# A hybrid mLSTM / HGRN2 decoder layer on one core: HGRN2 levels two to a step, a written order at the beginning, fewer products in the forget sums, a longer held tail

## The chip, the cores and the metric

The kernel runs on one core of a Trainium2 chip. The metric is the device time of one execution in microseconds, the median of several. The engines are named as in the profile: PE (matrix products and transposes; PEld is its weight load), DVE (vector), ACT (scalar), POOL (GpSimd) and SP, whose queue issues nearly all DMAs. Each engine takes its instructions in order.

## The reference, cut to what matters

One layer, 512 tokens, width 1024, all float32. One projection `x @ w_in` feeds two mixers; their gated sum goes through `w_out` and a layer norm, then a SwiGLU block (hidden 2816) and a second layer norm.

```python
def reference(...):
    u = x @ w_in[layer] + b_in[layer]
    (mq, mk, mv, mo, mi, mf, hq, hf, hi, hg, ga, gb) = jnp.split(u, split_points, axis=-1)
    h_a = _mlstm_chunkwise(...)        # 4 heads x 512, forget gate: running sum of log f over time
    h_b = _hgrn2_chunkwise(silu(hq), -expm1(log_f), hi, log_f)   # 8 heads x 128
    mixed = sigmoid(ga) * (h_a @ w_proj_a) + sigmoid(gb) * (h_b @ w_proj_b)
    x = _layernorm(ALPHA * x + mixed @ w_out, ln1_g, ln1_b)
    ffn = (silu(x @ w_ffn_gate) * (x @ w_ffn_up)) @ w_ffn_down
    x = _layernorm(ALPHA * x + ffn, ln2_g, ln2_b)

# HGRN2:  S_t = diag(f_t) S_{t-1} + k_t v_t^T,  k_t = 1 - f_t,  o_t = S_t^T q_t
```

## The kernel before

**Large products.** Every large product is made of three matmuls in a rounded float32 type (`mm3`: high by high, high by low, low by high), 128 x 512 each. `load_w` fetches a 512 KB piece of a weight into one of five `wraw` buffers, `split_w` makes its high part on ACT (`whi`) and its low part on DVE (`wlo`), in three buffers each. One projection (`proj_sub`) is 24 matmuls into one PSUM bank.

**Deferred work.** The rest of the computation is cut into pieces that are put between projections: `defer(n, fn)` keeps a piece back, `tick(w)` counts projections and runs what is due. The tool that builds the program then orders the instructions of each engine; `issue_after` and `keep_in_program_order` bind it.

**The beginning.** SP loads x as four row tiles `xn` with two pieces `rawv` of the value weights between them; PE transposes all four tiles (32 transposes, through PSUM tiles `px` and `s0` to `s2`), ACT and DVE split them into `xh` and `xl`, then `natural_part` makes the first values for four row tiles (96 matmuls of 264 columns).

**The mLSTM forget sums.** `gates_1` to `gates_4` run between the first projections. `gates_2` sums `lf` over time with ten float32 products of four columns (`tri` for a row tile itself, `ones` for each one before it); `gates_4` turns a running maximum (`mrow`) and makes the decay tables `dt`.

**HGRN2.** Two heads at a time (a pair, four in all), `h_units` makes f, K, Q and the output gate `og` by projections. `h_chain` then builds the scores by levels hs = 1, 2, 4, ... 256: at a level the keys of the lower half of each block of 2 hs tokens meet the queries of the upper half (`h_chunks` or the branches of `h_level`), `h_advance` multiplies the decay into half of Q and of K in place, and DVE's `copy_predicated` or ACT's copy puts the scores into `adc`, `ad`, `a1`, `a2`. The steps are due at 0 (the diagonal), 0.5, 1.25, 2, 2.75, 3.5, 4, 4.5, 5 and 5.5 ticks, the outputs (`h_out`) at 6 and 6.5. All these matmuls are float32, each two instructions in the trace: 32 x 32 or 32 x 16 in four column positions of the array for the diagonal and levels 1 to 16 (32 matmuls each), 32 x 32 in two positions for level 32 (16), 64 x 64 in one position for level 64 (8).

**The end.** `natural_pass` runs the last product for row tiles 2 and 3 over 22 weight rows k. The last three are held back (`tail=3`), so that the four PSUM banks end one after the other; `ln_stats` and `ln2_out` then do the layer norm by halves e of a row tile, one half of tile 2 on ACT and POOL.

## Time and profile before

| | us |
|---|---|
| median of 3 runs | 1318.94 (1315.4 to 1318.94) |
| the profiled execution, whole | 1315.66 |
| its span | 1313.9 |
| PE busy | 1297.1 (99%) |
| DVE busy | 709.9 (54%) |
| ACT busy | 528.5 (40%) |

The profiled execution takes 1.8 us outside the span; it is 3.3 us shorter than the median and close to the shortest run. PE's busy time counts pipelined instructions from their start to a modelled end, so a stall of a fraction of a microsecond shows in the distance from one start to the next and not as idle time. A 128 x 512 matmul starts 0.227 us after the one before it in the steady stretches.

### The profile page before, as it was taken

Reading aid. Unit: us, or ns where it says so; the run is one execution under the profiler, and the core shown is the slowest. Engines: PE = TensorE matmul, PEld = TensorE weight load, DVE = VectorE, ACT = ScalarE, POOL = GpSimd, SP = SyncE. Lnnn points to the kernel's source line nnn. Section 1 sums busy time; section 2 is a strip of 40 time slices with the busy share of each in tenths; the row PEclk is TensorE's granted clock in tenths of the full one; section 3 lists DMA queues with packets and bytes.
Section 4 is the critical chain, followed back from the end, with each engine's and each line's share of the span. In section 5 each row is a group of like instructions: output and inputs, shape, how many; then the busy total and the mean of one; then the engine's idle time right before and its main releaser. Section 6 shows DMA issues by size and latency. Waiting matters only on the chain.

```text
span 1313.9 us, 19136 instructions
## 1 busy us (share of the span) xinstructions
PE 1297.1 (99%) x7911; PEld 1091.0 (83%) x7911; DVE 709.9 (54%) x1104; ACT 528.5 (40%) x791; POOL 45.5 (3%) x100
## 2 busy tenths in 40 slices
PE   8999999999999999999999999999999999999997
PEld 7788888888888888888888888887898888888885
DVE  4765646566556664436464654255765533334565
ACT  4673544444343443224233334233863222223332
POOL 0010000000000000200000000000000000000001
PEclk9999999999999999999999999999999999999999
DMA  8222333233323332332332322326664333325562
GB/s 238 81 71 75 88 86 99 66 95 97 89 68 93 83 95 68 101 98 65 89 82 66 82 65 65 96 96 223 196 181 123 112 113 97 96 96 176 192 223 81
DMA packets 184023, 141.42 MB, mean 108 GB/s; under 512 B 5696, under 2 KB 167808, under 8 KB 183936
## 3 DMA queue, kind: packets, MB, share of 16 engines
q1 hardware_dynamic: 182880, 140.17, 36.6%
q8 instruction: 62, 1.02, 0.3%
q14 instruction: 25, 0.20, 0.1%
q10 hardware_dynamic: 1056, 0.03, 0.0%
HBM read 138.09 MB, written 2.10 MB: 107 GB/s over the span
## 4 chain that ended last, share of the span: by engine, by line
PE 97%; DVE 1%; ACT 1%; DMA 1%; issue 0%; POOL 0%; SPq 0%; DVEq 0%; POOLq 0%
PE pp L84 19%; PE pp L85 18%; PE pp L86 18%; PE pf L84 10%; PE pf L85 10%; PE pf L86 10%; PE px L698 1%; PE px L620 1%; PE px L84 1%; PE px L85 1%; PE px L86 1%; PE s L86 1%; PE s L85 1%; PE s L84 1%; DMA xn<-in_x_dram 1%; PE px L438 1%
## 5 line engine op out<-in xcount | busy, mean ns | idle before, releaser
L89 ACT CAST whi<-wraw 128x1024 fp32r<-128x1024 f32 x246 | 258.1, 1050 | 615.9 <-PE pp L85 249.4
L89 DVE TENSOR_TENSOR wlo<-wraw,whi 128x1024 fp32r<-128x1024 f32 x246 | 300.6, 1223 | 296.9 <-ACT whi L89 294.4
L84 PE MATMUL pp<-xh,whi 128*128 128x512 f32 x704 | 279.6, 397 | 0.0
L85 PE MATMUL pp<-xl,whi 128*128 128x512 f32 x704 | 275.5, 391 | 0.0
L86 PE MATMUL pp<-xh,wlo 128*128 128x512 f32 x704 | 275.4, 391 | 0.0
L86 PEld LDWEIGHTS pp<-xh,wlo 128*128 128x128 f32 x704 | 132.6, 188 | 28.4 <-issue 0.4
L84 PEld LDWEIGHTS pp<-xh,whi 128*128 128x128 f32 x704 | 132.5, 188 | 27.4 <-issue 1.0
L85 PEld LDWEIGHTS pp<-xl,whi 128*128 128x128 f32 x704 | 132.7, 189 | 26.0
L86 PE MATMUL pf<-x1h,wlo 128*128 128x512 f32 (+1 forms) x416 | 148.4, 357 | 0.7 <-DVE wlo L89 0.7
L84 PE MATMUL pf<-x1h,whi 128*128 128x512 f32 (+1 forms) x416 | 148.4, 357 | 0.0
L85 PE MATMUL pf<-x1l,whi 128*128 128x512 f32 (+1 forms) x416 | 148.3, 356 | 0.0
L86 PEld LDWEIGHTS pf<-x1h,wlo 128*128 128x128 f32 x416 | 78.6, 189 | 12.0 <-DVE wlo L89 0.9
L84 PEld LDWEIGHTS pf<-x1h,whi 128*128 128x128 f32 x416 | 78.6, 189 | 11.3
L85 PEld LDWEIGHTS pf<-x1l,whi 128*128 128x128 f32 x416 | 78.6, 189 | 11.3
L366 DVE SCALAR_TENSOR_TENSOR y<-u,cols,y 128x512 f32<-128x512 f32 x96 | 71.9, 750 | 6.1 <-ACT y L364 2.6
L85 PE MATMUL pf<-wlo,g 128*128 128x512 f32 x176 | 68.6, 390 | 0.0
L86 PE MATMUL pf<-whi,g 128*128 128x512 f32 x176 | 68.5, 389 | 0.0
L84 PE MATMUL pf<-whi,g 128*128 128x512 f32 x176 | 68.4, 389 | 0.0
L84 PE MATMUL pp<-whi,xh 128*128 128x512 f32 (+1 forms) x152 | 57.1, 375 | 0.0
L85 PE MATMUL pp<-wlo,xh 128*128 128x512 f32 (+1 forms) x152 | 56.1, 369 | 0.0
L86 PE MATMUL pp<-whi,xl 128*128 128x512 f32 (+1 forms) x152 | 55.9, 367 | 0.0
L84 PE MATMUL pp<-ht,whi 128*128 128x512 f32 x128 | 50.1, 391 | 0.0
(262 smaller groups left out, 1815.5 us busy)
## 6 DMA issues: line engine op xcount, KB each, us to landing
wraw<-in_w_in_dram SPq DMA_DIRECT2D x110, 512.0 KB, 3.9
wraw<-in_w_ffn_down_dram SPq DMA_DIRECT2D x44, 512.0 KB, 3.3
wraw<-in_w_ffn_gate_dram SPq DMA_DIRECT2D x26, 512.0 KB, 4.0
wraw<-in_w_ffn_up_dram SPq DMA_DIRECT2D x26, 512.0 KB, 3.9
wraw<-in_w_proj_a_dram SPq DMA_DIRECT2D x16, 512.0 KB, 3.5
wraw<-in_w_out_dram SPq DMA_DIRECT2D x16, 512.0 KB, 3.8
wraw<-in_w_proj_b_dram SPq DMA_DIRECT2D x8, 512.0 KB, 3.9
xn<-in_x_dram SPq DMA_DIRECT2D x4, 512.0 KB, 5.2
```

What stands on the lines that cost most here:

```text
L84: nc.tensor.matmul(ps, lh, rh, start=start, stop=False, **kw)
L85: nc.tensor.matmul(ps, lh, rl, start=False, stop=False, **kw)
L86: nc.tensor.matmul(ps, ll, rh, start=False, stop=stop, **kw)
L89: return nc.scalar.copy(hi, src), nc.vector.tensor_sub(lo, src, hi.bitcast(F32))
L366: nc.vector.scalar_tensor_tensor(y, u[:, tap:tap + T], cwcol(tap, ch), y, op0=OP.mult, op1=OP.add)
L438: nc.tensor.transpose(tps[:, i * P:(i + 1) * P], hn[:, i, c * P:(c + 1) * P], ident)
L620: nc.tensor.matmul(ps[32 * g:32 * g + 32, 4 * c + j], st["K"][:, c, cs], targets(st["Q"][:, c, cs]), start=True, stop=True, tile_position= ...
L698: nc.tensor.matmul(ops[:, i], at, vc(j), start=(e == 0), stop=(e == len(terms) - 1))
```

## The change

- **HGRN2.** The steps are now `h_first`, `h_step_0` (diagonal and level 1), `h_step_in` (levels 2 and 4, then 8 and 16), `h_step_32` (32 and 64) and `h_step_128` (128 and 256), due at 0, 0.5, 1.5, 2.5, 3.5 and 4.5 ticks. The first of two levels is advanced, its operands are copied by ACT (`h_keep`, into `f` and a new tile `qc`), the second is advanced too, and one tick later PE makes both levels together. The decayed queries stand in a tile of their own, `Q2`. Level 64 runs in two column positions, level 32 in four.
- **Beginning.** 13 transposes of the identity are issued first. The loads go x0, v0, x1, x2, v1, x3; `issue_after` writes out an order in which the value matmuls of tiles 0 and 1 (12 each) stand between the transposes. The splits of v go by halves.
- **Forget sums.** Two products of 16 columns (`tri` on `lf`, `ones` on the sums `az` that DVE adds up) in place of ten of four. `gates_4` is due one tick later and its second half is `gates_5`, half a tick later; the lower-bound arithmetic moves from `columns` to `gates_1`.
- **End.** Seven weight rows are held back instead of three, four of them in tiles `wend` of their own; both tiles' layer norm runs on DVE, tile 2's ahead of tile 3's.

The number of all other matmuls is the same.

```diff
+    for load, i in ((load_x, 0), (load_v, 0), (load_x, 1), (load_x, 2), (load_v, 1), (load_x, 3)):
+        load(i)
...
-    after((table,), lambda: transpose_x(0))
+    idle = psum(sp, "s2")
+    for i in range(13):
+        nc.tensor.transpose(idle[:, i % 4 * P:(i % 4 + 1) * P], ident, ident)
...
+    last = after((table,), lambda: transpose_x(0))
+    last = split_v(0, last)
+    last = after(last, lambda: transpose_x(1))
+    behind(last, lambda: first_values(0, 0))
+    last = after(done[-1:], lambda: after(last, lambda: transpose_x(2)))
+    last = split_v(1, last)
+    behind(last, lambda: first_values(1, 0))
+    last_x = after(done[-1:], lambda: after(last, lambda: transpose_x(3)))
+    for t, s_ in ((2, 0), (0, 1), (1, 1), (2, 1), (3, 0), (3, 1)):
+        behind(last_x, lambda: first_values(t, s_))
...
     def gates_2():
         bps = psum(px, "px", (P, NT, MH))
-        for i in range(NT):
-            for j in range(i + 1):
-                nc.tensor.matmul(bps[:, i], tri if j == i else ones, lf[:, j], start=(j == 0), stop=(j == i))
+        nc.tensor.matmul(bps.rearrange("p i h -> p (i h)"), tri, lf.rearrange("p i h -> p (i h)"), start=True, stop=False)
+        nc.tensor.matmul(bps.rearrange("p i h -> p (i h)"), ones, az.rearrange("p i h -> p (i h)"), start=False, stop=True)
...
-        defer(1, lambda: gates_4(mrow, mhl, sel))
+        defer(2, lambda: gates_4(mrow, mhl, sel))
...
+    def h_keep(st, hs):
+        nb = T // hs
+        kc, qc = st["f"], hp_.tile([P, 2, 256], F32, tag="qc", name="qc", bufs=1)
+        kk, qq = h_halves(st["K"], hs)[:, :, 0, :], h_halves(st["Q2"], hs)[:, :, 1, :]
+        if hs < 32:
+            nc.scalar.copy(h_halves(kc, hs)[:, :, 0, :], kk)
...
+        nc.scalar.copy(qc.rearrange("p c (b h) -> p (c b) h", h=hs), qq)
+        return kc, qc
...
+    def h_step_0(st):
+        ps = psum(px, "px", (P, 8, 48))
+        mm = h_chunks(ps[:, :, 32:48], st["K"], h_upper(st["Q2"], 1))
+        with tc.issue_after(mm.ins):
+            h_chunks(ps[:, :, 0:32], st["K"], lambda c, ch: st["Q"][:, c, 32 * ch:32 * ch + 32])
+        h_advance(st, 1)
+        st["kept"] = h_keep(st, 2)
+        nc.vector.copy_predicated(st["adc"], same.bitcast(U32)[:, None].to_broadcast([P, 8, 32]), ps[:, :, 0:32])
+        h_place(st, 1, ps[:, :, 32:48])
+        h_advance(st, 2)
...
+    def h_step_32(st):
+        kc, qc = st["kept"]
+        K, Q, ad = st["K"], st["Q2"], st["ad"]
+        ps = psum(px, "px", (P, 4, 96))
+        for n in range(4):
+            for i in range(2):
+                c, j = n // 2, 2 * (n % 2) + i
+                mm = nc.tensor.matmul(ps[64 * i:64 * i + 64, n, 0:64], K[:, c, j * P:j * P + 64],
+                                      Q[:, c, j * P + 64:(j + 1) * P], start=True, stop=True, tile_position=(0, 64 * i))
+        with tc.issue_after(mm.ins):
+            for n in range(4):
+                for i in range(2):
+                    for u in range(2):
+                        c, o, r = n // 2, (2 * (n % 2) + i) * 64 + 32 * u, 64 * u + 32 * i
+                        nc.tensor.matmul(ps[r:r + 32, n, 64:96], kc[:, c, o:o + 32], qc[:, c, o:o + 32],
+                                         start=True, stop=True, tile_position=(0, r))
...
-                  ((0.5, 1), (1.25, 2), (2, 4), (2.75, 8), (3.5, 16), (4, 32), (4.5, 64), (5, 128), (5.5, 256))]
+        steps = [(0, h_first), (0.5, h_step_0)]
+        steps += [(t, lambda st, hs=hs: h_step_in(st, hs)) for t, hs in ((1.5, 2), (2.5, 8))]
+        steps += [(3.5, h_step_32), (4.5, h_step_128)]
...
-                           lambda k, t: gl[k][:, 1, t * P:(t + 1) * P], ts_, tail=3 if ts_[0] else 0)
+                           lambda k, t: gl[k][:, 1, t * P:(t + 1) * P], ts_, tail=7 if final else 0, home=home)
```

PE at the very beginning, first before, then after (`xn` are tiles of x, `wvh`/`wvl` the split value weights):

```order
L209 MATMUL px<-ident,xn 128x128 x4
L209 MATMUL s_126<-ident,xn 128x128 x4
L209 MATMUL px<-ident,xn 128x128 x4
L209 MATMUL s_140<-ident,xn 128x128 x4
L209 MATMUL px<-ident,xn 128x128 x4
L209 MATMUL s_158<-ident,xn 128x128 x4
L209 MATMUL px<-ident,xn 128x128 x4
L209 MATMUL s_172<-ident,xn 128x128 x4
L84 MATMUL pp<-wvh,xh 128x264 x3
```

```order
L230 MATMUL s_119<-ident 128x128 x13
L217 MATMUL px<-ident,xn 128x128 x4
L217 MATMUL s_144<-ident,xn 128x128 x4
L217 MATMUL px<-ident,xn 128x128 x4
L217 MATMUL s_164<-ident,xn 128x128 x4
L86 MATMUL pp<-wvh,xh 128x264
L87 MATMUL pp<-wvl,xh 128x264
```

The value matmuls now start behind the second tile of x and the transposes of the other two tiles stand among them, 12 matmuls apart.

PE in the first pair of HGRN2, level 64 before, then levels 64 and 32 after, each with the projections around it:

```order
L84 MATMUL pp<-xh,whi 128x512
L85 MATMUL pp<-xl,whi 128x512
L86 MATMUL pp<-xh,wlo 128x512
L651 MATMUL px<-Q,K 64x64 x8
L84 MATMUL pp<-xh,whi 128x512
L85 MATMUL pp<-xl,whi 128x512
L86 MATMUL pp<-xh,wlo 128x512
```

```order
L86 MATMUL px<-whi,xh 128x512
L87 MATMUL px<-wlo,xh 128x512
L88 MATMUL px<-whi,xl 128x512
L731 MATMUL px<-Q_4675,K 64x64 x8
L738 MATMUL px<-qc,f 32x32 x16
L86 MATMUL pp<-xh,whi 128x512
L87 MATMUL pp<-xl,whi 128x512
L88 MATMUL pp<-xh,wlo 128x512
```

The 16 matmuls of level 32 have left their own place, 17 projection matmuls earlier, and stand right behind level 64.

DVE in the first pair around the diagonal and levels 1 and 2, before, then after (`adc` takes the scores, `tot` are products of f):

```order
L627 TENSOR_TENSOR Q<-Q,f 128x1024
L628 COPY_PREDICATED adc_4448<-same,px 128x256
L605 TENSOR_TENSOR Q<-Q,f 128x512
L606 TENSOR_TENSOR K<-K,f 128x512
L670 COPY_PREDICATED adc_4448<-mask_4396,px 128x128
L89 TENSOR_TENSOR wlo<-wraw,whi 128x1024
L605 TENSOR_TENSOR Q<-Q,tot 128x256x2
L606 TENSOR_TENSOR K<-K,tot 128x256x2
L670 COPY_PREDICATED adc_4448<-mask_4404,px 128x64x2
```

```order
L642 TENSOR_TENSOR Q_4675<-Q_4675,f 128x512
L91 TENSOR_TENSOR wlo<-wraw,whi 128x1024
L643 TENSOR_TENSOR K<-K,f 128x512
L702 COPY_PREDICATED adc_4462<-same,px 128x256
L642 TENSOR_TENSOR Q_4675<-Q_4675,tot 128x256x2
L682 COPY_PREDICATED adc_4462<-mask_4410,px 128x128
L643 TENSOR_TENSOR K<-K,tot 128x256x2
```

The two advances now follow each other with one weight split between them, where before PE had a visit between them.

## Rows read from the trace of the kernel before

**Rows 1.** The page: busy time by engine, then the chain by engine.
```profile
PE 1297.1 (99%) x7911; PEld 1091.0 (83%) x7911; DVE 709.9 (54%) x1104; ACT 528.5 (40%) x791; POOL 45.5 (3%) x100
PE 97%; DVE 1%; ACT 1%; DMA 1%; issue 0%; POOL 0%; SPq 0%; DVEq 0%; POOLq 0%
```

**Rows 2.** Timeline of PE, HGRN2 stage: start, duration, line, operation, count.
```profile
576.11 0.39 PE L86 MATMUL px<-whi,xl 128*128 128x512 f32 x1
576.43 0.74 PE L620 MATMUL px<-Q,K 128*32 128x16 f32 x64
577.09 0.50 PE L84 MATMUL pp<-whi,xh 128*128 128x512 f32 x1
577.43 0.39 PE L85 MATMUL pp<-wlo,xh 128*128 128x512 f32 x1
...
598.85 0.70 PE L645 MATMUL px<-Q,K 128*32 128x32 f32 x32
599.48 0.50 PE L85 MATMUL pp<-xl,whi 128*128 128x512 f32 x1
...
603.56 1.15 PE L651 MATMUL px<-Q,K 128*64 128x64 f32 x16
604.63 0.50 PE L84 MATMUL pp<-xh,whi 128*128 128x512 f32 x1
```

**Rows 3.** Timelines of DVE and ACT at the first pair's level-1 visit.
```profile
577.22 0.69 DVE L605 TENSOR_TENSOR Q<-Q,f 128x512 f32<-128x512 f32 x1 [3.45 <-PE px L620]
578.43 0.44 DVE L670 COPY_PREDICATED adc<-mask,px 128x128 f32<-128x128 uint32 x1
578.65 1.26 DVE L89 TENSOR_TENSOR wlo<-wraw,whi 128x1024 fp32r<-128x1024 f32 x1
576.53 1.05 ACT L89 CAST whi<-wraw 128x1024 fp32r<-128x1024 f32 x1 [4.93 <-PE px L86]
```

**Rows 4.** Timeline of PE, forget sums; square brackets: idle before, releaser.
```profile
41.82 0.28 PE L306 MATMUL px<-gs,tri 128*128 128x4 f32 x2
...
43.97 0.48 PE L84 MATMUL pp<-xh,whi 128*128 128x512 f32 x1
...
59.63 0.38 PE L329 MATMUL px<-ident,mrow 4*128 4x4 f32 x4 [0.55 <-DVE mrow L317]
```

**Rows 5.** One stretch: length, busy us by engine, granted TensorE clock, DMA share, GB/s.
```profile
45.00:48.00 3.00, 3.00 (x9) 2.35 (x8) 2.98 (x6) 1.96 (x3) 0.00 (x0) 0.50 0.30 88
```

**Rows 6.** Timeline of PE at the beginning.
```profile
5.03 1.09 PE L209 MATMUL px<-ident,xn 128*128 128x128 f32 x4 [5.03 <-DMA xn<-in_x_dram]
...
9.62 1.08 PE L209 MATMUL px<-ident,xn 128*128 128x128 f32 x4 [0.94 <-DMA xn<-in_x_dram]
10.50 1.06 PE L209 MATMUL s<-ident,xn 128*128 128x128 f32 x4
...
13.72 0.38 PE L85 MATMUL pp<-wvl,xh 128*128 128x264 f32 x1
13.94 0.29 PE L86 MATMUL pp<-wvh,xl 128*128 128x264 f32 x1
14.07 0.29 PE L84 MATMUL pp<-wvh,xh 128*128 128x264 f32 x1
...
25.08 0.40 PE L84 MATMUL pp<-xh,whi 128*128 128x512 f32 x1
```

**Rows 7.** First value weights: issue on SP; times to landing of rawv's four transfers.
```profile
1.71 0.43 SPq L199 DMA_DIRECT2D rawv<-in_w_in_dram  x1
DMA to landing us min/median/max: 4.3/6.6/8.7
```

**Rows 8.** The end: PE's last matmul, then two instructions of DVE (timelines).
```profile
1305.03 0.39 PE L86 MATMUL pf<-whi,g 128*128 128x512 f32 x1
1305.15 0.75 DVE L877 SCALAR_TENSOR_TENSOR z<-z,lsm,lnb 128x512 f32<-128x512 f32 x1
1306.42 0.67 DVE L770 SCALAR_TENSOR_TENSOR z<-x,pf 128x512 f32<-128x512 f32 x1
```

More of the change, by code (lines that the diff above doesn't have):

```diff
@@ L80, in tile_hybrid_trunk @@
     pp = pool(st_pp, "pp", bufs=3, space=PSUM, side="right")
+    done = []
     def mm3(ps, lh, ll, rh, rl, start, stop, **kw):
@@ L85, in mm3 @@
         nc.tensor.matmul(ps, lh, rl, start=False, stop=False, **kw)
-        nc.tensor.matmul(ps, ll, rh, start=False, stop=stop, **kw)
+        done.append(nc.tensor.matmul(ps, ll, rh, start=False, stop=stop, **kw))
     def split(src, hi, lo):
@@ L299, in gates_1 @@
         nc.vector.tensor_sub(lf, t1, ln_u)
+        nc.vector.memset(az[:, 0], 0.0)
+        for i in range(1, NT):
+            nc.vector.tensor_add(az[:, i], az[:, i - 1], lf[:, i - 1])
         defer(1, gates_2)
@@ L356, in feature_chunk @@
         off = (O_MK if w == 0 else O_MQ) + h * MD + c * P
-        wh, wl = split_w(first[w] if h + c == 0 else load_w(in_cols(off), KD, P))
+        if h + c == 0:
+            wh, wl = after(last_x, lambda: split_w(first[w]))
+        else:
+            wh, wl = fetch(in_cols(off), KD, P)
         ps = proj_sub(wh, wl, 0, xh, xl)
@@ new lines, in h_step_in @@
+    def h_step_in(st, hs):
+        kc, qc = st["kept"]
+        ps = psum(px, "px", (P, 2, 8, 16))
+        mm = h_chunks(ps[:, 1], st["K"], h_upper(st["Q2"], 2 * hs))
+        with tc.issue_after(mm.ins):
+            h_chunks(ps[:, 0], kc, h_packed(qc))
+        h_advance(st, 2 * hs)
+        st["kept"] = h_keep(st, 4 * hs)
+        for e in range(2):
+            h_place(st, hs << e, ps[:, e])
+        h_advance(st, 4 * hs)
+        if hs == 8:
+            for g in range(4):
+                rows_ = slice(32 * g, 32 * g + 32)
+                nc.scalar.copy(st["ad"][rows_, :, 32 * g:32 * g + 32], st["adc"][rows_])
@@ L655, in h_level, with h_step_128 @@
+    def h_step_128(st):
+        kc, qc = st["kept"]
+        K, Q = st["K"], st["Q2"]
+        for c in range(2):
+            lps = psum(px, "px", (P, 2, 256))
+            for b in range(2):
+                mm = nc.tensor.matmul(lps[:, b], K[:, c, b * P:(b + 1) * P], Q[:, c, 256:512], start=True, stop=True)
+            nc.scalar.copy(st["a2"][:, c], lps)
+        lps = psum(px, "px", (P, 2, 2, P))
+        with tc.issue_after(mm.ins):
             for c in range(2):
                 for b in range(2):
-                    nc.tensor.matmul(lps[:, c, b], K[:, c, 2 * b * P:(2 * b + 1) * P],
-                                     Q[:, c, (2 * b + 1) * P:(2 * b + 2) * P], start=True, stop=True)
-        else:
-            for c in range(2):
-                lps = psum(px, "px", (P, 2, 256))
-                for b in range(2):
-                    nc.tensor.matmul(lps[:, b], K[:, c, b * P:(b + 1) * P], Q[:, c, 256:512],
-                                     start=True, stop=True)
-                nc.scalar.copy(st["a2"][:, c], lps)
-            return
@@ L685, in h_out @@
+        nc.scalar.copy(st["a1"], lps)
     def h_out(st, c):
@@ L778, in ln_small, with natural_pass, step @@
         return lp.tile([P, 20], F32, tag="lsm", name="lsm", bufs=4)
[L780 removed]
+    def natural_pass(wsrc, nk, lhs_h, lhs_l, ts_, tail=0, home=None):
         pss = {t: [psum(pf, "pf") for _ in range(2)] for t in ts_}
         last = []
[L784 to L786 removed]
+        def step(k, t, cs, wh, wl):
+            e, c0 = cs.start // 512, cs.start % 512
+            mm3(pss[t][e][:, c0:c0 + cs.stop - cs.start], lhs_h(k, t), lhs_l(k, t), wh[:, 0, cs], wl[:, 0, cs],
+                k == 0, k == nk - 1, skip_group_check=bool(tail))
         for k in range(nk):
[L789 to L790 removed]
+            raw = load_w(wsrc[k * P:(k + 1) * P, :], 1, D)
+            i = k - (nk - tail)
+            if 0 <= i < 4:
+                wh, wl = (part[:, i:i + 1] for part in home)
+                split(raw, wh, wl)
+            else:
+                wh, wl = split_w(raw)
+            if i >= 0:
                 last.append((k, wh, wl))
@@ L793, in natural_pass @@
             for t in ts_:
-                for e in range(2):
-                    step(k, t, e, wh, wl)
+                for es in HALF:
+                    step(k, t, es, wh, wl)
             tick(0.5)
-        for t in ts_:
-            for e in range(2):
+        for n, t in enumerate(ts_):
+            for cs in HALF:
                 for k, wh, wl in last:
-                    step(k, t, e, wh, wl)
+                    step(k, t, cs, wh, wl)
         return pss
```

182 lines of the change are left out of this document (78 added, 104 removed).

## Prediction

> **What bounds the kernel now.** The page comes first: PE is busy for 99% of the span and carries 97% of the chain that ends last, while DVE has 54% and ACT 40% [rows 1]. So a microsecond taken off PE's stream is a microsecond off the end, and work for DVE or ACT costs nothing as long as PE doesn't wait for it. Second, the timeline of PE, read from start to start: durations there overlap, and a lost tenth of a microsecond shows only in the distance to the next start. A 128 x 512 matmul takes 0.227 us that way. Third, the granted clock, for places at which PE runs at half pace without being idle. I sum against the profiled execution (1315.66 us; 1313.9 of span and 1.8 around it). The median is 1318.94, 3.3 above it; the shortest run 1315.4. So if the new runs lie as the old median does, 3.3 is to be added, and the range must hold that.
>
> **HGRN2: fewer visits.** Between projections PE makes short float32 visits. At level 1 the last projection matmul starts at 576.11 and would be done with its slot at 576.34; the visit starts at 576.43, ends at 577.09, and the next matmul takes 0.34 instead of 0.227 [rows 2]. So a visit costs 0.09 to enter and 0.11 to leave, 0.20 us, beside 0.66 for its 64 instructions. Before, a pair makes eight such visits (diagonal, levels 1 to 64), now four with the same matmuls: 4 x 0.20 = 0.8 us. Levels 128 and 256 change places with the output; there a visit is joined and another split, which I count as nothing.
>
> **HGRN2: side by side.** Level 64 takes 604.63 - 603.56 = 1.07 us for 16 instructions in one column position, 67 ns each; level 32 takes 0.63 for 32 in two positions, 20 ns each; level 1 runs in four positions at 0.66 / 64 = 10 ns [rows 2]. Level 32 moves to four: 32 x 10.5 = 0.34, a gain of 0.29. Level 64 moves to two. Its lower bound is half of 1.07, 0.53, and its upper bound is that nothing overlaps, 1.07; doubling level 32's 20 ns for double the columns gives 16 x 39 = 0.63. I take 0.57, near these two, a gain of 0.5. A pair gains 0.8 + 0.29 + 0.5 = 1.6 us, four pairs 6.4. In the last pair some visits already stood side by side with the outputs of the pair before, one more than now will, so 6.3 (bounds 4.3 and 6.8).
>
> **What hides the copies.** Each step now waits for two advances and two ACT copies. In the order of DVE after the first step stand: Q times f, a weight split, K, `adc`, Q, `adc`, K. With Q and K at 0.69, the split at 1.26 and `adc` at 0.44 [rows 3] that is 4 x 0.69 + 1.26 + 2 x 0.44 = 4.9 us; the first can start when the first half of the visit is done, 0.7 before its end, so the last ends 4.2 behind the visit, some 4.5 with the hand-overs. The split doesn't hold it up: its ACT part started at 576.53, with the visit, and took 1.05 [rows 3]. The copies (512 columns, about half of that 1.05 each) run under the split and `adc`. PE meanwhile has 24 projection matmuls, 5.4 us. So PE comes 0.9 us later than its data and the term is nothing; without that cover it would be paid in full, 16 times.
>
> **Forget sums.** The ten products are 20 instructions from 41.82 to 43.97, 2.15 us, 107 ns each [rows 4]. The two new ones are four, 0.43, in two visits, one more entry and exit (0.2): gain 1.5. Right behind them the granted clock is 0.50 from 45 to 48 us, the lower level of 1.2 GHz, with PE busy throughout [rows 5]; what PE did before it fell were those 2.15 us of four-column products. With them gone I expect no fall; half of 3.0 us is 1.5 (bounds 0 and 1.7).
>
> **The running maximum.** PE idles 0.55 us before the transposes of `mrow` [rows 4]; due one tick later, they find it done: 0.6 with the start of the stream. Against it, the new `lf` product stands behind the same 48 matmuls as the old ones while its Exp and Ln now follow the first two chunks on ACT; a wait of up to 0.6 there is possible, so the bounds are 0 and 0.7.
>
> **The beginning.** Transposes wait until 5.03 for the first tile of x, and 0.94 us at 9.62 for the third; four take 0.88 us, and the 264-column matmuls first start 0.22 apart (1.2 GHz), from 13.94 on 0.121 (91 of them from 14.07 to 25.08) [rows 6]. The rise came 4.3 us after the unbroken run of PE began at 9.62. Now x1 is the third transfer; the third one landed at 1.71 + 6.6 = 8.3 before [rows 7]. So the unbroken run begins at 8.43: eight transposes to 10.2, 12 matmuls at 0.22 to 12.8, where after the same 4.3 us the pace doubles; then x2 0.88, 12 matmuls 1.45, x3 0.88, 72 matmuls 8.7: 24.7 against 25.08, a gain of 0.4. If the 13 idle transposes have the clock up before x1, PE is at 9.6 with the split of v, and the sum ends near 23.0: gain 2.1. If the rise comes only at 16, it ends at 26.3: a loss of 1.2. I take 0.4, which counts nothing for the idle transposes. The Trainium skill, page "TensorE: Matmul & The Clock Gate", section "Part 4: PE-mode transpose", says that transposes don't count as a busy PE for the clock. By that the idle ones are without effect, and the sum is 1304.4 at best; were it wrong, 1302.5. The trace can't tell: the rise came behind 3.3 us of transposes and 1 us of matmuls.
>
> **The end.** PE's last matmul ends at 1305.42, but DVE turns to its last PSUM bank only at 1306.42, since it is still at tile 2 (1305.15) [rows 8]. With seven rows held back each bank takes 21 matmuls, 4.8 us, instead of nine; tile 2's eight instructions of 0.67 to 0.75 us [rows 8], some 5.7, are then done before PE ends. DVE starts at once: gain 0.95 (bounds 0.5 and 1.0). The held weights cost nothing: the last one's buffer comes free as the tail starts, its splits take 1.05 + 1.26 us [rows 3], and PE needs it 18 matmuls later, 4.1 us.
>
> **Sum.** 6.3 + 1.5 + 1.5 + 0.6 + 0.4 + 0.95 = 11.25 us: 1315.66 - 11.25 = **1304.4**.
>
> **Rival 1, the clock keeps its own time.** The fall at 45 us stays, since float32 visits remain there, and the rise at the beginning comes late: 1.5 + 0.4 + 1.2 lost, 1307.5. For it: I know one fall and one rise only. Against it: the four-column stretch is the only one of its kind.
>
> **Rival 2, level 64 doesn't overlap.** Then 4 x 0.5 is lost: 1306.4. Against it: level 32 against level 1 shows overlap in two and four positions. The Trainium skill, same page, section "Part 3: Packing small matmuls — row/col tiling", has weight loads overlap running matmuls only where the row groups differ, and column positions share theirs; that would be this case. Level 1's 10 ns an instruction, loads among them, speak against it.
>
> **Rival 3, PE waits a little at every step.** If hand-overs or queued adds bring the 4.5 us to 5.9, each of the 16 intervals (four a pair) costs 0.5: 8 us, 1312.4, no change that could be told (0.3%, 4 us, is about what a measurement here can tell).
>
> **Rival 4, slower.** The same place, priced higher: the chain of two advances and two copies lasts 6.6 us, since ACT's in-order queue puts a copy behind a weight cast that itself waits for PE. Then PE waits 1.2 us 16 times, 19 us: 1323.6. It is slower than before by 0.3% from about 1.0 us a wait on, that is, from a chain 2 us longer than the one summed. Against it: DVE has 46% of the span free.
>
> **How the numbers follow.** Forecast 0.64 (1301.5 to 1306.5 by its bounds), rival 1 0.14, rival 2 0.09, rival 3 0.08, rival 4 0.05. Faster by over 0.3%: 0.64 + 0.14 + 0.09 = 0.87; within: 0.08; slower: 0.05. The range goes from the bounds' lower side, 1300.5, to rivals 1 and 2 with part of the median's 3.3, 1309.
>
> **What would show it.** Four tile visits a pair with no idle time before them, the 64 x 64 group at about 0.57 us, no stretch at clock 0.5 near 45 us, no wait before the `mrow` transposes, the first 512-column matmul at about 24.7, DVE's last bank within 0.1 us of PE's end. Idle time before `L670` or `L738` would prove rivals 3 and 4.

## The result and the profile after

The changed kernel takes 1303.2 us in the median (1302.4 to 1303.9), measured between runs of the kernel before with a median of 1317.2. The ratio is 0.9905, 95% interval 0.989 to 0.992. Beside the experiments it was timed again: 1303.75 us, ratio 0.9904 (0.989 to 0.992). Forecast were 1304.4, between 1300.5 and 1309: the time and the sign came out as predicted. The terms behind the sum did so only in part, and most of what follows is about those that did not.

The profiled execution took 1303.77 us, with a span of 1302.0 (before 1315.66 and 1313.9), so 11.9 us were gained between these two. Busy time by engine and the chain by engine, answering to [rows 1]:

```profile
PE 1287.7 (99%) x7908; PEld 1086.5 (83%) x7908; DVE 709.7 (55%) x1111; ACT 550.7 (42%) x838; POOL 43.0 (3%) x98
...
PE 93%; ACT 3%; DVE 2%; issue 1%; DMA 0%; POOL 0%; SPq 0%; DVEq 0%; POOLq 0%; ACTq 0%
```

PE is still the bound. The chain has 1% of "issue" now, time in which PE stood still with nothing to wait for; it had 0% before.

PE's timeline in the HGRN2 stage of the first pair, answering to [rows 2] (start, duration, engine, line, operation, tiles, count):

```profile
577.46 0.39 PE L88 MATMUL px<-whi,xl 128*128 128x512 f32 x1
577.77 0.72 PE L670 MATMUL px<-Q,K 128*32 128x16 f32 x63
...
578.34 0.73 PE L670 MATMUL px<-qc,f 128*32 128x16 f32 x62
579.00 0.50 PE L86 MATMUL pp<-whi,xh 128*128 128x512 f32 x1
...
591.57 0.69 PE L731 MATMUL px<-Q,K 128*64 128x64 f32 x16
592.18 0.46 PE L738 MATMUL px<-qc,f 128*32 128x32 f32 x32
592.57 0.50 PE L86 MATMUL pp<-xh,whi 128*128 128x512 f32 x1
```

A visit of two levels has 128 matmuls and lasts 579.00 - 577.77 = 1.23 us where two visits had 0.66 each. Level 64 takes 592.18 - 591.57 = 0.61 us (before 1.07), level 32 takes 0.39 (before 0.63). No square bracket stands at these rows: PE does not wait for the steps. DVE's part of the first step in that pair ends with this instruction:

```profile
575.16 0.73 DVE L643 TENSOR_TENSOR K<-K,tot 128x512 f32<-128x512 f32 x1
```

It ends at 575.89, 3.8 us behind the end of the visit (572.09), and the next visit starts at 577.77, so 1.9 us are to spare; 0.9 were predicted.

Forget sums and running maximum, answering to [rows 4] (timeline of PE):

```profile
40.36 0.29 PE L338 MATMUL px<-gs,tri 128*128 128x16 f32 x2
...
43.83 0.37 PE L339 MATMUL px<-gs,ones 128*128 128x16 f32 x2
...
60.10 0.41 PE L362 MATMUL px<-ident,mrow 4*128 4x4 f32 x4
```

The stretch that had the lower clock, answering to [rows 5] (length, busy us by engine in the order PE, PEld, DVE, ACT, POOL, granted clock, DMA share, GB/s):

```profile
45.00:48.00 3.00, 3.00 (x16) 2.24 (x15) 2.50 (x6) 1.58 (x3) 0.00 (x0) 1.00 0.65 170
```

Two short visits stand where one long one was, nothing is waited for ahead of the transposes of `mrow`, and the stretch runs at 1.00, with 16 matmuls where it had 9.

The beginning, answering to [rows 6] (PE's timeline):

```profile
1.53 3.03 PE L230 MATMUL s<-ident 128*128 128x128 f32 x13 [1.53 <-POOL ident masks.py:199]
4.88 1.12 PE L217 MATMUL px<-ident,xn 128*128 128x128 f32 x4 [0.32 <-DMA xn<-in_x_dram]
...
7.98 1.11 PE L217 MATMUL px<-ident,xn 128*128 128x128 f32 x4 [1.13 <-DMA xn<-in_x_dram]
...
10.63 0.40 PE L87 MATMUL pp<-wvl,xh 128*128 128x264 f32 x1
10.85 0.31 PE L88 MATMUL pp<-wvh,xl 128*128 128x264 f32 x1
10.99 0.28 PE L86 MATMUL pp<-wvh,xh 128*128 128x264 f32 x1
11.11 0.28 PE L87 MATMUL pp<-wvl,xh 128*128 128x264 f32 x1
...
23.63 0.40 PE L86 MATMUL pp<-xh,whi 128*128 128x512 f32 x1
```

Up to 10.85 the starts are 0.22 apart, from 10.99 on 0.12: the clock rose from 1.2 to 2.4 GHz there. (The profile's granted clock reads 1.00 before the first rise too, so that the distance of the starts has to tell it.) The first 512-column matmul starts at 23.63 instead of 25.08.

The end, answering to [rows 8] (PE's last matmul, then DVE's turn to its PSUM bank):

```profile
1294.09 0.39 PE L88 MATMUL pf<-whi,g 128*128 128x512 f32 x1
...
1294.51 0.69 DVE L851 SCALAR_TENSOR_TENSOR z<-x,pf 128x512 f32<-128x512 f32 x1 [3.34 <-PE pf L88]
```

DVE turns to the bank 0.03 us after PE is done; it was 1.0 late. From PE's end to the end of the span are 1302.0 - 1294.48 = 7.5 us, before 1313.9 - 1305.42 = 8.5.

Behind the beginning, two waits of PE are new (list of PE's waits: releaser, us in total, times, longest):

```profile
PE pp L86 <- issue: 1.6, 1, 1.6
...
PE pp L87 <- DVE wlo L91: 0.5, 1, 0.5
```

The first stands in the last pair's HGRN2 stage (PE's timeline):

```profile
761.45 0.66 PE L792 MATMUL px<-ident,on 128*128 128x128 f32 x4
763.72 0.50 PE L86 MATMUL pp<-xh,whi 128*128 128x512 f32 x1 [1.62 <-issue]
```

"Issue" says that the matmul at 763.72 waited for nothing that the profile shows. What ends shortly before is a DMA packet of another kind than the kernel's own. The list of DMA queues has, for the whole run (queue, kind: packets, MB, share)

```profile
q8 instruction: 62, 1.02, 0.3%
```

and for 760.5 to 763 us

```profile
q8 instruction: 1, 0.02, 2.7%
```

62 packets of 16 KB stand beside 7908 matmuls and 7908 weight loads, 255 instructions to a packet. So the first theory on the stall was that these packets bring PE its program, block by block, and that PE ran out of instructions.

### The profile page after: what moved, and what is told of

Same layout as the page of the kernel before. It is cut to its first block, busy times and chain, and to the rows that moved or that the text cites. A ratio compares the mean times of both kernels' runs of the same rounds, so it can differ in the third digit from the quotient of the medians.

```text
span 1302.0 us, 19166 instructions
## 1 busy us (share of the span) xinstructions
PE 1287.7 (99%) x7908; PEld 1086.5 (83%) x7908; DVE 709.7 (55%) x1111; ACT 550.7 (42%) x838; POOL 43.0 (3%) x98
## 4 chain that ended last, share of the span: by engine, by line
PE 93%; ACT 3%; DVE 2%; issue 1%; DMA 0%; POOL 0%; SPq 0%; DVEq 0%; POOLq 0%; ACTq 0%
PE pp L86 18%; PE pp L88 18%; PE pp L87 18%; PE pf L88 9%; PE pf L86 9%; PE pf L87 9%; PE px L779 1%; PE px L670 1%; PE px L87 1%; PE px L88 1%; PE px L86 1%; PE s L87 1%; PE s L88 1%; PE s L86 1%; ACT xt L909 1%
## 5 line engine op out<-in xcount | busy, mean ns | idle before, releaser
L91 ACT CAST whi<-wraw 128x1024 fp32r<-128x1024 f32 x242 | 253.7, 1050 | 588.1 <-PE pp L87 261.4
L91 DVE TENSOR_TENSOR wlo<-wraw,whi 128x1024 fp32r<-128x1024 f32 x242 | 295.5, 1223 | 289.5 <-ACT whi L91 286.9
L86 PE MATMUL pf<-whi,g 128*128 128x512 f32 x160 | 62.2, 389 | 0.0
L87 PE MATMUL pf<-wlo,g 128*128 128x512 f32 x160 | 62.2, 389 | 0.0
L88 PE MATMUL pf<-whi,g 128*128 128x512 f32 x160 | 62.2, 389 | 0.0
```

The source lines that it names most:

```text
L86: nc.tensor.matmul(ps, lh, rh, start=start, stop=False, **kw)
L87: nc.tensor.matmul(ps, lh, rl, start=False, stop=False, **kw)
L88: done.append(nc.tensor.matmul(ps, ll, rh, start=False, stop=stop, **kw))
L91: return nc.scalar.copy(hi, src), nc.vector.tensor_sub(lo, src, hi.bitcast(F32))
```

## Experiments

Each took the changed kernel and altered one thing, except where it says otherwise. Times are medians unless one execution is named. The kernel before was timed beside every group of experiments (1315.1 to 1315.2), the changed kernel only at first (1303.2) and beside the last group (1303.75). Differences of one or two microseconds between experiments are therefore read from the traces, not from the medians alone.

**Without the idle transposes.** Edit:

```
-    for i in range(13):
-        nc.tensor.transpose(idle[:, i % 4 * P:(i % 4 + 1) * P], ident, ident)
```

> The changed kernel without its 13 idle transposes; nothing else differs, so PE's instruction stream after the start is 26 instructions shorter (13 weight loads, 13 matmuls). Clock, theory A (the idle transposes do nothing for the clock): the first pace of 0.12 us per 264-column matmul again at about 10.9 us, first 512-column matmul at 23.6, time 1303.2. Theory B (they brought the rise forward, since it came 2.9 us after the last gap and not 4.3 as in the kernel before): the rise comes 4.3 us after 7.98, at 12.3, the first 512-column matmul at 24.2 to 24.4, time 1303.9. The 1.6 us in which PE stands still at 762 us without a semaphore wait: theory C (instruction blocks of 256 instructions arrive late when a block's border falls at a visit's start) says that the stall moves or goes, because the borders lie 26 instructions further on in the stream; theory D (visits that stand next to outputs and transposes are too dense wherever the borders are) says that it stays at the same instruction with 1 to 2 us.

Measured: 1302.13 us, 1.1 to 1.6 less than with them. The clock rose at 11.2 us and the first 512-column matmul started at 23.75, so in the profile after, with its rise at 10.9, the 13 transposes had been worth 0.12 us (where the rise came early, below, it is 1.6). What made the kernel faster was the stall. Compared at the same projection matmul, this trace is 0.1 us behind the profile after at 24 us, 0.3 behind it at 748 and 1.6 ahead of it from 781 on. In PE's waits

```profile
PE px L667 <- issue: 0.3, 1, 0.3
```

is all that is left of "issue", and it stands at 722 us, in another visit. 26 instructions fewer at 2 us take away a stall of 1.6 us at 762, where nothing was changed: theory C, the borders of instruction blocks.

**The same idle time with ordinary matmuls.** Edit:

```
-    for i in range(13):
-        nc.tensor.transpose(idle[:, i % 4 * P:(i % 4 + 1) * P], ident, ident)
+    for i in range(7):
+        nc.tensor.matmul(idle[:, i % 4 * P:(i % 4 + 1) * P], ident, ident, start=True, stop=True)
```

> The 13 idle transposes become 7 ordinary float32 matmuls of the same 128 x 128 tile, about the same 3 us of PE from 1.5 on. Theory A (transposes don't count for the clock, matmuls do): the rise comes earlier than 10.87 us, as early as about 6, so that the eight transposes of x1 and the first value matmuls run at the higher pace and the first 512-column matmul starts at 22.3 to 23.2; time 1302 to 1302.8. Theory B (what comes before the waits for x at 4.9 and 8.0 us is of no account, transposes or not): rise at 10.9, first 512-column matmul at 23.6, time 1303.2. A third outcome, matmuls slower than thought so that x0 is delayed, would show as the first transpose of x0 after 4.9.

Measured: 1303.78 us, no gain. The clock rose at 4.67, as theory A has it, then fell again at 8.08, behind 2.03 us in which PE stood idle waiting for x1, and came back at 11.5; the first 512-column matmul started at 23.94. Two stretches (length, busy us by engine, granted clock, DMA share, GB/s):

```profile
4.80:8.00 3.20, 1.14 (x9) 0.86 (x8) 1.78 (x3) 2.24 (x4) 0.00 (x0) 1.00 1.09 368
8.20:11.40 3.20, 3.20 (x16) 3.20 (x16) 1.92 (x3) 1.17 (x2) 0.00 (x0) 0.50 1.06 369
```

Neither theory had an early rise that is lost again. An execution with the transposes did just the same (below), so between these two the kind of work made no difference.

**Level 64 one position after the other.** Edit:

```
-        for n in range(4):
-            for i in range(2):
+        for i in range(2):
+            for n in range(4):
```

> In the step of levels 32 and 64 the eight products of level 64 are issued tile by tile of one column position and then those of the other, so neighbours no longer stand in different positions (except once); the same instructions otherwise. Theory A (side by side means that two neighbours in different column positions overlap): the 16 matmuls take 67 ns each again, 1.07 us instead of 0.61, +0.4 to 0.46 us a pair, time 1303.2 + 1.7 = 1304.9. Theory B (the rate doesn't depend on the neighbour's position): 0.61 us stays, 1303.2. The stall of 1.6 us at 762 us should be there again in both, as the stream has the same length, if it hangs on the borders of instruction blocks.

Measured: 1303.51 us. The visit's timeline:

```profile
590.22 0.97 PE L731 MATMUL px<-Q,K 128*64 128x64 f32 x16
591.12 0.46 PE L738 MATMUL px<-qc,f 128*32 128x32 f32 x32
591.51 0.50 PE L86 MATMUL pp<-xh,whi 128*128 128x512 f32 x1
```

0.90 us, 56 ns a matmul: 0.29 more than in the changed kernel (38 ns), but less than the 67 ns of before. The single starts in the trace say why. In the kernel before, neighbours in the one position start 58 to 59 ns apart, and so they do in this run, but for three of its distances, which are 4 to 6 ns; in the changed kernel every other distance is 6 to 7 ns. So the order of this run still had three places at which the next matmul started at once, as between different positions, and these three are the 0.17 us by which it beats the kernel before. Overlap between neighbours in different positions then accounts for all of level 64's gain, 0.46 us a pair, of which this run took back 0.29. The stall was at the same instruction.

**The last pair two projections later.** Edit, in `h_chain`:

```
-                defer(t, lambda step=step: step(st))
+                defer(t + 2 * (st["pr"] == 3), lambda step=step: step(st))
```

> In the last pair of heads all steps after the first are due two projections later, so its first visits no longer stand next to the outputs and transposes of the pair before. Theory C (borders of instruction blocks): no visit of over 256 instructions is left in that place, so a block border at a visit's start is needed for a stall; the 1.6 us at 762 us go, a smaller one of about 0.3 may be left elsewhere. Theory D (dense visits): the stall goes too, since no visit is dense. Both 1303.2 - 1.6 + 2 x 0.2 (two visits that stood joined now pay their own entry and exit) = 1302.0. Theory E (something else, such as a late weight split or an accident of that execution): the stall stays near 762 or was not in most executions, 1303.2 to 1303.6.

Measured: 1301.41 us, 1.8 to 2.3 less. (The profiled execution is 3.0 below the profile after; 1.5 of that is an early rise of the clock, at 6.1 us.) No "issue" is left at 762, 0.37 us at 721. That fits theories C and D alike; the run without idle transposes, where the visits were as dense as ever, tells them apart.

**The ten products back.** Edit: the two products of `gates_2` replaced by the loop of the kernel before.

> The changed kernel with the ten float32 products of the forget sums back in the place of the two. Theory A (those four-column products are what the clock falls behind): the visit takes about 2.3 us again instead of 0.6, +1.7, and behind it the granted clock falls to 0.50 for some 3.4 us, +1.7; time 1303.2 + 3.4 = 1306.6. Theory B (the fall at 45 us in the kernel before had to do with its beginning or with chance): +1.7 alone, clock 1.00 throughout, 1304.9. The stream of PE is 32 instructions longer behind 40 us, so the borders of instruction blocks stand elsewhere: by the theory of borders the 1.6 us at 762 us are not at the same instruction; if they go, 1.6 less than both figures.

Measured: 1305.9 us. Compared at the same projection matmul, the products and a longer wait behind them (0.8 for 0.5 us at 85 us) cost 2.2 us between 24 and 122 us; the fall of theory A did not come, another did. Three stretches of this kernel (length, busy us by engine, granted clock, DMA share, GB/s):

```profile
41.30:44.70 3.40, 3.40 (x16) 2.83 (x17) 3.27 (x7) 1.79 (x3) 0.00 (x0) 1.00 0.05 4
45.00:48.00 3.00, 3.00 (x15) 2.57 (x14) 2.96 (x6) 1.84 (x3) 0.00 (x0) 1.00 0.94 274
764.00:767.00 3.00, 3.00 (x21) 2.58 (x14) 2.54 (x6) 1.14 (x2) 0.00 (x0) 0.50 0.02 5
```

Behind the ten products (39.03 to 41.25) the clock stayed up. It fell at 764, behind a stall of 2.1 us:

```profile
PE px L671 <- issue: 2.1, 1, 2.1
```

So the products don't always have a fall behind them, and a stall for instructions can. Whether the products bear on it at all was left to a run on the kernel before (below).

**The old levels.** The HGRN2 code of the kernel before, one level to a step, in the changed kernel (the edit, long, is that part of the change taken back).

> The changed kernel with the nine-step HGRN2 levels of the kernel before; beginning, gates and end as changed. Theory A (the prediction's term): 6.3 us come back, 1303.2 + 6.3 = 1309.5. Theory B (by the trace the visits themselves got 7.8 us shorter and 1.9 went to stalls for instructions, which the old order doesn't have): the same sum near 1309.1 if the stall is counted in, and no idle PE between 570 and 800 us in this kernel's trace. Theory C (part of the gain of the whole is not the levels' but the copies' and order's elsewhere): under 1307.5.

Measured: 1309.37 us, and no "issue" among PE's waits. So the levels are worth 5.6 to 6.2 us net, close to the forecast of 6.3, and theory B says what that is made of: the time by which all visits of the stage set the projections back (0.227 us a projection matmul taken off) is 62.4 us with the old levels and 56.4 with the new ones, and 54.3 in a kernel with the new ones and no stall (the last experiment).

**Gates sooner.** Edits: `defer(2, ...)` for `gates_4` back to `defer(1, ...)`, and `gates_5` called at once.

> Stabiliser transposes one projection sooner and the stabiliser's products in the same visit again, as in the kernel before; the rest as changed. Theory A (the new wait of 0.5 us at 84 us comes from the 16 exponentials and their masks now standing half a tick later, before the weight splits of the value projection): that wait goes, and the wait of 0.55 us before the transposes of mrow comes back; the sum is within 0.3 us of the changed kernel. Theory B (the 0.5 us at 84 us come from the value projection's weights themselves): it stays, and with the mrow wait the span gets about 0.6 longer.

Measured: 1303.82 us in one execution. PE's waits have both:

```profile
PE pp L87 <- DVE wlo L91: 1.1, 1, 1.1
...
PE px L362 <- DVE mrow L350: 0.7, 1, 0.7
```

The wait for the value projection's weights did not go away, it grew; the one for `mrow` came back. Theory A falls, theory B holds as far as it goes: the 0.5 us are the smaller form of something that the sooner gates make worse. The total hides this, since this execution had an early rise of the clock (6.3): compared at the same projection matmul it was 1.5 us ahead of the profile after at 24 us and 0.4 behind it at 122. So the sooner gates cost 1.9 us, and the later ones are the better place.

**A delay beside the chain.** 48 products of a scratch tile on DVE:

```
+    def h_delay(st):
+        for _ in range((2, 4, 6, 0)[st["pr"]]):
+            nc.vector.tensor_mul(dly, dly, dly)
...
+        h_delay(st)
         h_advance(st, 1)
...
```

> Extra DVE work (in-place products of a 512-column scratch tile, about 0.61 us each) ahead of the first advance of each of a pair's first four steps: two in the first pair (1.2 us), four in the second (2.4), six in the third (3.7), none in the last. Theory A (the prediction's chain: 4.5 us against 5.4 of cover, 0.9 us spare at every step): PE waits 0.3 at each of four visits of the first pair, 1.5 in the second, 2.8 in the third, in all 18 us. Theory B (the spare time that the trace of the changed kernel shows: 1.9, 3.1, 2.9 and 2.2 us at the four visits of the first two pairs, 1.0, 2.3, 2.9 and 2.7 in the third): nothing in the first pair, 0.5 + 0.2 in the second, 2.7 + 1.4 + 0.8 + 1.0 = 5.9 in the third, in all 6.6 us. Theory C (DVE queues the weight splits behind the delay and PE waits for weights as well): over 8 us.

Measured: 1306.25 us in one execution, but it tells nothing on the chain. All instructions of that line, with first and last start:

```profile
L700 DVE TENSOR_TENSOR dly<-dly x48: 676/692/752, 520.1 to 571.5; 128x512 f32<-128x512 f32 x48
```

Nothing depended on them, and the tool that builds the program put them ahead of the steps that they were to delay. PE waited for DVE no more than in the changed kernel. The time has the late rise (10.78), the stall (1.66 us) and a fall of the clock behind it (765.1 to 768.5) in it.

**A delay within the chain.** The same with an operand that the chain needs:

```
+        for _ in range((1, 3, 4, 0)[st["pr"]]):
+            nc.vector.tensor_scalar_mul(st["Q2"], st["Q2"], 1.0)
```

> Extra DVE work in the chain itself: at each of a pair's first four steps the query tile is multiplied by 1.0 (1024 columns, about 0.9 us) before its first advance, once in the first pair, three times in the second, four times in the third, not in the last. Theory A (the prediction's 0.9 us to spare): nothing in the first pair, 1.8 us of waiting at each of four visits in the second, 2.7 in the third: 18 us. Theory B (what the trace of the changed kernel has to spare at the four visits: 1.9, 3.1, 2.9, 2.2 us in the first two pairs and 1.0, 2.3, 2.9, 2.7 in the third): nothing in the first pair, 0.8 + 0.5 in the second, 2.6 + 1.3 + 0.7 + 0.9 in the third: 6.8 us. Over 10 with waits for weights among them would mean that the delay also pushes back the weight splits behind it on DVE.

Measured: 1306.05 us in one execution. The 32 extra instructions took 22.1 us of DVE, and PE's wait for them was

```profile
PE px L670 <- DVE Q L642: 0.3, 1, 0.3
```

in all. Neither theory had that. The order shows why: in the third pair 39, 29, 29 and 36 projection matmuls now stand between one visit and the next, where 24 stood, so the tool that builds the program had set the visits further apart. (One of these products took 0.69 us, not 0.9.) The rest of the time above the changed kernel's is the clock: it rose at 4.71 behind nothing but the 13 transposes, fell at 8.13, rose at 11.54, and fell once more behind the stall, from 765.9 to 769.3.

**The kernel before with two products.** The only experiment on the kernel before: the two products of the change in `gates_2`, with the running sums that they need.

> The kernel before with one thing changed: the forget sums by two products instead of ten. Theory A (the ten four-column products lie ahead of every fall of the clock, which comes or doesn't come with their place against the instants at which the clock is set; in the kernel with ten products and the new beginning it didn't come): 1.5 us less in every execution, the clock falls at 45 us in none, and the spread of the times, 1313.8 to 1318.9 in the kernel before, shrinks to what the beginning leaves, about 1.5; median 1312.4, highest 1314. Theory B (the falls have another cause): 1.5 us less but the spread stays, executions of up to 1317 among them, and a mean granted clock as low as 0.994.

Measured over 11 executions: 1313.87 us (1313.36 to 1315.61), none with a mean granted clock under 0.996. The kernel before beside it, 15 executions: two of 1313.6 and 1313.9, eight of 1314.9 to 1315.4 and five of 1316.7 to 1318.6, these five at a mean of 0.994. This speaks for theory A: no long execution is left without the ten products, with five in 15 (12 in 35 over all groups of runs) against none in 11; but none of the long ones was profiled. Theory A's figures were too good: it had 1314 as the highest time and a spread of 1.5, where 1315.6 and 2.3 came. The median gained only 1.35 us (ratio 0.9988, 0.998 to 0.9997), less than the 1.85 us by which the visit got shorter, because two of PE's waits, 0.55 and nothing before, take 1.2 of it back, and a third, new, 0.2:

```profile
PE px L331 <- DVE mrow L319: 1.2, 1, 1.2
...
PE s L84 <- ACT kq L89: 0.6, 1, 0.6
...
PE s L85 <- DVE kq L89: 0.2, 1, 0.2
```

Without the later due time PE just arrives at `mrow` earlier; the two edits belong together.

**The changed kernel again.**

> The changed kernel once more, unchanged, beside the others. By the runs so far its clock rises at 6.1 to 6.7 us in some executions and at 10.8 to 10.9 in others, with the first 512-column matmul at 22.1 or 23.6; so two groups of times, 1302.4 and 1303.8, and in all of them a stall of 1.3 to 1.7 us near 762 us that begins at the same instruction. If the stall were an accident of single executions it would be missing here or be elsewhere.

Measured: 1303.75 us (1303.2 to 1304.0). The stall was there, at the same instruction. The clock rose at 5.2 us, and the first 512-column matmul started at 22.11, yet this execution took 1304.04, because of what came behind the stall (PE's timeline, then the stretch behind it):

```profile
762.38 0.50 PE L86 MATMUL pp<-xh,whi 128*128 128x512 f32 x1 [1.67 <-issue]
...
763.35 0.63 PE L86 MATMUL pp<-xh,whi 128*128 128x512 f32 x1
763.78 0.63 PE L87 MATMUL pp<-xl,whi 128*128 128x512 f32 x1
```

```profile
763.00:766.30 3.30, 3.30 (x9) 2.57 (x8) 2.57 (x4) 0.62 (x1) 0.00 (x0) 0.50 0.07 12
```

From 763 to 766.3 the clock is granted at 0.50, and starts are 0.43 apart instead of 0.227: 1.7 us more. So two things move the times of the changed kernel from execution to execution, and here they offset each other: an early rise gains 1.5, a fall behind the stall takes 1.7.

**Both causes removed.** The last pair later, and eight more idle transposes in PE's wait for x1:

```
+    def fill():
+        for i in range(8):
+            turned.append(nc.tensor.transpose(idle[:, i % 4 * P:(i % 4 + 1) * P], ident, ident))
+
+    after(turned[-1:], fill)
+    last = after(turned[-1:], lambda: after(last, lambda: transpose_x(1)))
```

> The last pair's steps two projections later, and eight more idle transposes between those of x0 and x1, where PE waits for x1. Theory A (transposes raise the clock like other work, and the late rise comes where too much idle time lies before it): the rise comes by 7.6 us in every execution, the first 512-column matmul at 22.0 to 22.6, the times keep to one group near 1300.8; with the borders of instruction blocks 16 instructions further on, the 0.37 us at 721 us go as well, 1300.4. Theory B (transposes don't count): rises at 6.2 and 10.9 as before, 1300.8 to 1302.2. If the eight transposes run at the lower clock beyond the arrival of x1, the transposes of x1 start at 8.2 instead of 7.9 and 0.2 us are lost.

Measured: 1300.12 us, all executions between 1299.97 and 1300.23, ratio to the kernel before 0.9878 (0.9865 to 0.9892). This beats both kernels, and its spread is 0.26 us where that of the changed kernel was 1.5. With the last pair later alone it was 1301.41 with a spread of 1.3. The beginning (PE's timeline):

```profile
5.56 1.06 PE L217 MATMUL s<-ident,xn 128*128 128x128 f32 x4
6.42 1.12 PE L258 MATMUL s<-ident 128*128 128x128 f32 x8
7.81 0.66 PE L217 MATMUL px<-ident,xn 128*128 128x128 f32 x4 [0.27 <-DMA xn<-in_x_dram]
8.30 0.60 PE L217 MATMUL s<-ident,xn 128*128 128x128 f32 x4
8.66 0.37 PE L86 MATMUL pp<-wvh,xh 128*128 128x264 f32 x1
8.86 0.28 PE L87 MATMUL pp<-wvl,xh 128*128 128x264 f32 x1
```

The clock rose at 6.59, and all value matmuls run 0.12 apart. "Issue" is not among its waits at all. That is theory A, as far as one profile and four times can show it.

**Where the stall stands.** Put together, the traces place it to the instruction. Counted in matmuls from the visit's start, PE stopped after 132 in both profiles of the changed kernel and in four others whose stream has the same length up to there. With 16 matmuls more ahead (ten products) it stopped after 116, with one more (seven matmuls, recorded as 14, for 13 transposes) after 131. The small stall at 721 us stood after 106 matmuls, with one more ahead after 105, with 13 fewer after 119. Counted from the start of the program the place is the same in all runs that have it: 5188 matmuls are recorded ahead of the long stall, 4678 ahead of the small one. Between the two lie 510 matmuls, 509 weight loads and 5 other instructions of PE, 1024 in all, four times 256. And in each case PE went on 1.3 to 1.5 us after a 16 KB instruction packet had come in. That the stop is at the border of a block of 256 instructions is shown by this; why some blocks come late is not. A visit of 128 matmuls and 128 weight loads uses up a whole block in 1.23 us, which projections need 29 us for, but not every such visit stalled.

## Why the prediction was right, point by point

**The sum** was 11.25 us, the two profiled executions differ by 11.9. The pieces, read from the trace one by one: beginning 1.45, forget sums 1.7, clock at 45 us 1.7, running maximum and stabiliser 1.15 less 0.65 for the new wait and its restart, levels 5.9 with the stall counted in, end 0.95: 12.2. Where the 0.3 too much lies shows when the same projection matmul is compared in both traces: the changed kernel is 1.45 us ahead at the first, 4.67 at 122 us, 10.74 at 812, 10.94 at PE's last matmul and 11.9 at the end. So forget sums, clock and running maximum gave 3.2 together (forecast 3.6) and not 3.9, and the levels 6.1; which of the three pieces is too large stays open. That the sum came so near is in part luck: the beginning gave 1.05 more than its term, the three behind it 0.4 less, and the levels hide two larger errors.

**Levels, forecast 6.3, measured 5.9 (5.6 to 6.2 by the experiment).** Right in size, wrong in its parts. A pair without a stall gained 2.2 us, not 1.6. Entering and leaving is as computed, 0.21 a visit, 0.85. Levels 32 and 64 together gained 0.70 (forecast 0.79: 0.61 and 0.39 where 0.57 and 0.34 stood). Two things were not in the sum: 128 matmuls in one visit take 1.23 and not 1.33, presumably since the start of a visit is paid once (0.35 in three visits), and levels 128 and 256 with the output were counted as nothing and gave 0.25. Against these stood the stalls for instructions, 1.6 to 2.1 us, for which no row of the kernel before gave a hint: there "issue" was 0% [rows 1]. Without the stalls the levels would have given about 8 (62.4 to 54.3). The forecast hit because two errors of like size cancelled.

**What hides the copies.** The step "PE comes 0.9 us later than its data" was too cautious in the first pair, 1.9 us, and about right in the third, where the last K ends at 713.03 and the next visit starts at 714.07, 1.0 later. More important, it asked the wrong question. With up to 2.8 us of DVE work added to each step, PE waited 0.3 us in all, since the tool that builds the program sets the visits further apart when the chain gets longer. Rivals 3 and 4 (waits of 0.5 or 1.2 us at 16 steps) did not come: no such wait is among PE's. Probably they would have needed a chain longer than that tool reckons with; no run shows that.

**Forget sums, forecast 1.5:** 2.31 us for the visit before, 0.24 and 0.35 for the two of after, 1.7.

**The clock at 45 us, forecast 1.5:** it didn't fall there, and the gain was there in the profile. But the step "what PE did before it fell were those products", so without them no fall, was half of it. It fell behind the ten products in the profile of the kernel before and did not in that of the changed kernel with ten products. Rival 1 had the fall at 45 stay, which it didn't; but its idea, that a fall can come with other work, proved right at a place that the prediction had not looked at: behind the stall at 762 us, in four of the eight profiles that had it. Its price there, 1.7 us, is that of the fall at 45.

**The running maximum, forecast 0.6:** the wait is gone, and the four groups of `gates_5` with the transposes take 3.6 us of PE where they had 4.8. Of these 1.15 the wait of 0.5 at 84 us takes back more than half. The bounds (0 to 0.7) held for the net figure.

**The beginning, forecast 0.4, measured 1.45 and 3.0 (first 512-column matmul at 23.63 and 22.11).** This term failed, at the step that lets the rise come 4.3 us after the unbroken run of PE begins and counts nothing for the idle transposes. In the profile after, that run began at 7.98 and the rise came 2.9 us later; without the idle transposes it came 3.2 later (7.96 and 11.17). In nine profiles with the 13 transposes the clock rose at 4.7 to 6.7 us in seven, of which one lost it again, and at 10.8 and 10.9 in two. In the seven PE had done nothing but transposes by then. The Trainium skill, page "TensorE: Matmul & The Clock Gate", section "Part 4: PE-mode transpose", says that transposes don't count as a busy PE for the clock. Here they do, and in the two profiles that can be set side by side they do so like matmuls: with transposes it rose at 4.71, fell at 8.13 and was back at 11.54, with ordinary matmuls in their place at 4.67, 8.08 and 11.5. The measurement decides. The prediction named 1302.5 for this case and set it aside on that rule. Its gain for the case, 2.1, was too low as well: with the early rise the value matmuls began at 8.64, not at 9.6, and 3.0 were gained.

**The end, forecast 0.95:** 0.95, with DVE 0.03 us behind PE.

**Rival 2, level 64 doesn't overlap:** refuted by 38 ns a matmul in alternating positions against 56 in one position after the other (58 between neighbours in the same position). The rule of the Trainium skill that stood behind it (page "TensorE: Matmul & The Clock Gate", section "Part 3: Packing small matmuls — row/col tiling": weight loads overlap running matmuls only between different row groups) doesn't hold for this case. All these matmuls use all 128 rows, and in the trace nearly all their weight loads start 2 to 3 ns after the matmul ahead of them, in the kernel before too.

**The median's 3.3 us.** The prediction added them to the range without a cause. The ten products are the likely one: among the 11 executions without them none was above 1316 us. That falls of the clock made the long ones so is argued from their mean granted clock (0.994), not seen in a trace.

## What to carry over

When many tiny instructions are packed into one visit, count them against the blocks in which an engine's program arrives (256 instructions here), and look for idle time with no releaser: such a stall moves with every instruction added or removed anywhere ahead of it, so that an edit that should be neutral can be worth 1.6 us, and another 1.7 if the clock falls behind the stall. Before trusting a difference of a few microseconds, compare the clock's rises and falls in both traces; filling PE's waits at the beginning with idle work, beside the last pair's later steps, made the kernel faster and its times repeat within 0.3 us. Adding a delay to learn what a chain has to spare only works if the order stays as it was.

## What was not expected of the hardware

- PE stood still for 1.35 to 2.1 us at a border of instruction blocks. The Trainium skill, page "Runtime: NRT & Kernel Launch", section "Instruction fetch mechanics", has blocks of 16 KiB, 256 instructions, fetched ahead, and the cost of a border as mostly hidden. 62 packets of 16 KB for 15,816 instructions agree with the size; in visits of 128 matmuls in 1.23 us the cost is not hidden.
- A stall of that kind can be followed by 3.4 us at 1.2 GHz (granted 0.50) although PE is busy again from its end on. It came behind the four longest stalls (1.66 to 2.12 us) and not behind the four shortest (1.35 to 1.62); at the beginning, a wait of 1.8 us for x1 had no fall behind it, so the length alone does not decide.
- An early rise of the clock was lost again in two profiles in which PE then waited 2.0 and 2.1 us for x1 (4.67 up and 8.08 down, 4.71 up and 8.13 down); in six in which it waited 1.2 to 1.8 it stayed.
- Sixteen 64-column matmuls take 0.61 us with neighbours in different column positions and 0.90 with neighbours mostly in the same; there, starts are 58 ns apart.
